# Grouping an expert's token transposes by the rows that they read

## The chip, the cores and the metric

The kernel runs on one core of one Trainium2 chip. The metric is the device time of one execution in microseconds (us). TensorE (PE) multiplies and transposes, with its weight loads recorded apart (PEld); VectorE (DVE) and ScalarE (ACT) read its results out of PSUM; GpSimd (POOL) issues the gathers and scatters; SyncE (SP) issues the large loads.

## The reference

One decoder layer over 2048 tokens of width 1024: attention and a gated recurrence side by side, an output projection, and then a sparse layer of 32 experts. Each token goes to two experts. For an expert with weights `w_gate`, `w_up` (1024 x 512) and `w_down` (512 x 1024):

```
hid = silu(xb @ w_gate[e]) * (xb @ w_up[e])
y   = (hid @ w_down[e]) * gate
out[token] += y
```

Everything is float32. Only the expert layer is touched by the change.

## The kernel before, in words

The first 1375 us or so are projections, attention, the recurrence and the routing. The rest, `phase_c`, walks over the 32 experts in an order `E[0]`, `E[1]`, ... that is fixed by `even_order`: expert number r of the size ranking has room for `CAPS[r]` tokens. Nineteen of the 32 entries of `CAPS` are over 128 (from 132 to 192), thirteen are 128. `E[0]` has 176. So `E['tails']` is one block of 128 rows for thirteen experts, and for nineteen a block of 128 rows and a second block of w = `CAPS[r]` - 128 rows, from 4 to 64.

For each expert these things happen, and the lines are those of the profile:

- `expert_in` (L1687): POOL gathers the tokens' rows from memory, the first 128 into `xg0` and the w behind them into `xg1`. Each of these tiles has one buffer, so a gather waits until the transposes of the expert before have read it. `E[0]` alone takes buffers of the name `eH`.
- `expert_x` (L1701 to L1706): PE transposes the rows, 128 columns at a time, eight such blocks (`KT` = 8) of each tile, into a PSUM tile `tr` of one bank with two buffers. ACT copies it into `xs` (L1704), DVE subtracts that from the bank to get the rest (L1705), and makes the bf16 copy `xb` (L1706). All three are needed by the expert's matmuls.
- `weights_up` (L1645, L1654, L1660) and `weights_down` (L1676): SP loads twelve pieces of 512 KB; the eight of gate and up land in `eraw` (six buffers), ACT makes `eH` of each and DVE the rest `eL` (eleven buffers each).
- `expert_up`: the gate and up matmuls, in four quarters. For an expert of over 128 tokens the weights are the stationary operand (L1727, L1724), otherwise the tokens are (L1745 to L1747).
- `expert_hid`, `expert_down`, `expert_out` (L1764, L1777 or L1789, L1822, L1829): the down projection, transposes back for the larger experts, and a scatter that adds into memory.

The order of PE's instructions is written out by hand: `manual_schedule` keeps them in the order in which the program issues them. After each quarter of `expert_up(E[r])` one step of the outstanding `expert_out` and one step of `expert_x(E[r + 1])` are issued, so the transposes of the next expert lie between the quarters of the present one:

```
for _ in self.expert_up(E[r]):
    next(out, None)
    next(x, None)
for _ in x:
    pass
```

Then come the gather of the expert after next, the down projection of the expert before, and the loads of weights. ACT, DVE, POOL and SP are ordered by the framework's planner, by the program's order, with the expert functions moved up by 250 places (`soon`), and by its own estimate of when an operand is there.

Of the kernel before, what the change touches and what calls it, by code (L numbers as in the profile page):

```python
# [9 lines left out]
F32 = mybir.dt.float32  # L10
# [5 lines left out]
AF = mybir.ActivationFunctionType  # L16
# [7 lines left out]
KT = DM // 128  # L24
# [140 lines left out]
class Layer:  # L165
# [1525 lines left out]
    @soon  # L1691
    def expert_x(self, E):
        nc, cap = self.nc, E['cap']
        xs = E['xs'] = self.mx.tile([128, KT, 2, cap], F32R, name="xs", bufs=2)
        xb = E['xb'] = self.mx.tile([128, KT, cap], BF16, name="xb", bufs=2)
        for k2 in range(KT // 2):
            pt = self.psm.tile([128, 2, 256], F32, name="tr", bufs=2)
            for j in range(2):
                k = 2 * k2 + j
                for i, w in E['tails']:  # L1700
                    nc.tensor.transpose(pt[:, j, 128 * i:128 * i + w], E['xg'][i][:, 128 * k:128 * k + 128],  # L1701
                                        self.c['ident'][0:w, 0:w])
            ks = slice(2 * k2, 2 * k2 + 2)
            nc.scalar.activation(xs[:, ks, 0, :], pt[:, :, 0:cap], AF.Copy)  # L1704
            nc.vector.tensor_sub(xs[:, ks, 1, :], pt[:, :, 0:cap], xs[:, ks, 0, :].bitcast(F32))  # L1705
            nc.vector.tensor_copy(xb[:, ks, :], xs[:, ks, 0, :].bitcast(F32))  # L1706
            yield

    @soon
# [212 lines left out]
```

## Time and profile before

| | |
|---|---|
| time, median of 3 runs | 2245.28 us (2243.73 to 2248.41) |
| the profiled execution | 2245.75 us, span 2243.9 us |
| mean granted clock of PE | 0.946 of full |
| PE | 2000.7 us busy (89%), 13777 instructions |
| PEld | 1356.6 us (60%) |
| DVE | 1500.7 us (67%), 4211 instructions |
| ACT | 1209.6 us (54%), 2691 instructions |
| POOL | 545.0 us (24%) |
| memory | 305.30 MB read, 66.29 MB written |

Busy times are shares of the whole span and mix stages with different limits. In the page's forty slices of some 56 us PE reads 9 or more from the 26th to the 38th, and DMA reads 8 or 9 there, while DVE and ACT read 5 to 7. A busy PE is not PE at its peak, since the ends of its pipelined instructions are modelled; what it could have left out is read from the distances between starts.

### The profile page before, as it was taken

To read this page: it belongs to the slowest core of one execution; us is meant where nothing else is said; L and a number is where in the kernel's file an instruction comes from. 1 tells how busy PE (TensorE), PEld (TensorE's weight loads), DVE (VectorE), ACT (ScalarE), POOL (GpSimd) and SP (SyncE) were. 2 spreads that over 40 slices of the span, in tenths; PEclk is the share of its full clock that TensorE was granted. 3 is DMA by queue.
4 is the path that set the end of the run, shared out by engine and by line. 5 is a ranking of instruction groups with operands and counts; after the bars stand their busy time and mean duration, and the time that the engine had idled before them with its cause. 6 is when DMAs were issued, how large, how long until landed. Compare 5 with 4: busy or idle time off the path is not lost. (4 is left out here: it accounts for less than half of the span.)

```text
span 2243.9 us, 39874 instructions
## 1 busy us (share of the span) xinstructions
PE 2000.7 (89%) x13777; PEld 1356.6 (60%) x13777; DVE 1500.7 (67%) x4211; ACT 1209.6 (54%) x2691; POOL 545.0 (24%) x620
## 2 busy tenths in 40 slices
PE   5998978999899998998888896999999999999981
PEld 4645565555755557554544444779999977766750
DVE  7657686778767696568876677665566656556525
ACT  6455653765547555666653433645555555555524
POOL 2312244033522235213331113021122321111110
PEclk9998988999999999999899996999999999999995
DMA  7234254533445235634579995899888999999857
GB/s 232 79 94 103 62 128 108 120 87 77 117 109 135 56 92 144 155 90 112 121 213 251 268 226 167 297 300 291 298 286 280 314 314 302 313 343 310 287 149 297
DMA packets 438896, 433.37 MB, mean 193 GB/s; under 512 B 242644, under 2 KB 325716, under 8 KB 438176
## 3 DMA queue, kind: packets, MB, share of 16 engines
q1 hardware_dynamic: 420464, 382.74, 55.8%
q0 software_dynamic: 14064, 46.46, 8.7%
q8 instruction: 108, 1.77, 0.3%
q10 hardware_dynamic: 4160, 1.58, 0.3%
q14 instruction: 100, 0.82, 0.1%
HBM read 305.30 MB, written 66.29 MB: 166 GB/s over the span
## 5 line engine op out<-in xcount | busy, mean ns | idle before, releaser
L1660 DVE TENSOR_TENSOR eL<-eraw,eH 128x1024 bf16<-128x1024 f32 x248 | 297.8, 1220 | 120.0 <-ACT eH L1654 114.5
L1654 ACT ACTIVATE eH<-eraw 128x1024 fp32r<-128x1024 f32 x252 | 258.5, 1053 | 110.5 <-PE acc L1746 59.0
L453 ACT ACTIVATE P<-S,orow,fqk 128x256 f32<-128x256 f32 (+1 forms) x384 | 195.2, 513 | 172.7 <-DVE orow L447 87.4
L567 PE MATMUL proj<-whh,x 128*128 128x512 f16 x512 | 202.6, 396 | 0.1
L568 PE MATMUL proj<-whl,x 128*128 128x512 f16 x512 | 201.2, 393 | 0.0
L569 PE MATMUL proj<-whh,x 128*128 128x512 f16 x512 | 199.9, 390 | 0.0
L1727 PE MATMUL acc<-xs,eH 128*128 128x352 f32 (+15 forms) x1216 | 196.0, 314 | 0.5 <-DVE xs L1705 0.5
L436 PE MATMUL S<-k,qs 128*128 128x256 f16 (+1 forms) x768 | 171.9, 355 | 14.1 <-ACT P L453 11.4
L1727 PEld LDWEIGHTS acc<-xs,eH 128*128 128x128 f32 x1216 | 176.1, 190 | 4.4 <-issue 2.4
L440 DVE CUSTOM_DVE_ANT_0 S<-S,bias 128x256 f32<-128x256 f32 (+1 forms) x384 | 141.3, 368 | 53.9 <-PE S L436 50.6
L456 DVE TENSOR_TENSOR Ps<-P,Ps 128x256 f16<-128x256 f32 (+1 forms) x192 | 130.6, 680 | 68.0 <-ACT Ps L455 65.1
L1829 POOL DMA_INDIRECT x2d<-yo,sidx x49 | 83.8, 1711 | 378.7 <-ACT xs L1704 98.1
L1777 PE MATMUL acc<-hs,eD 128*128 128x176 f32 (+15 forms) x1216 | 165.9, 296 | 1.1 <-DVE ts L1752 0.7
L1777 PEld LDWEIGHTS acc<-hs,eD 128*128 128x128 f32 x1216 | 160.5, 190 | 2.0 <-DVE ts L1752 1.0
L436 PEld LDWEIGHTS <-qs 128*128 128x128 f16 x768 | 89.2, 123 | 70.4 <-issue 22.8
L260 POOL TENSOR_TENSOR wraw<-wraw,g 128x1024 f32<-128x1024 f32 x44 | 84.8, 1929 | 167.2 <-DMA wraw<-in_w_in_dram 150.6
L1687 POOL DMA_INDIRECT xg<-h2d,gidx x49 | 54.7, 1117 | 268.8 <-PE tr L1701 249.0
L1745 PE MATMUL acc<-eH,xs 128*128 128x512 f32 x208 | 119.3, 574 | 0.0
L1789 PE MATMUL acc<-eD,hs 128*128 128x512 f32 x208 | 99.3, 616 | 20.5 <-ACT hs L1765 9.9
L386 PE MATMUL proj<-wh,x 128*128 128x128 f16 x512 | 95.0, 229 | 19.2 <-DVE V L394 19.2
L455 ACT ACTIVATE Ps<-P 128x256 f16<-128x256 f32 (+1 forms) x192 | 102.8, 535 | 6.0 <-DMA PT<-Ps 3.3
L658 POOL TENSOR_SCALAR sw<-Sp,hw 128x128 f32<-128x128 f32 x112 | 53.5, 478 | 197.0 <-DVE Sp L661 107.6
(396 smaller groups left out, 4960.4 us busy)
## 6 DMA issues: line engine op xcount, KB each, us to landing
eraw<-in_w_gate_dram SPq DMA_DIRECT2D x128, 512.0 KB
eD<-in_w_down_dram SPq DMA_DIRECT2D x128, 512.0 KB
eraw<-in_w_up_dram SPq DMA_DIRECT2D x124, 512.0 KB
wraw<-in_w_in_dram SPq DMA_DIRECT2D x41, 512.0 KB
od<-orow SPq DMA_DIRECT2D x64, 132.0 KB
R<-od SPq DMA_DIRECT2D x64, 132.0 KB
xt<-in_x_dram SPq DMA_DIRECT2D x16, 512.0 KB
wraw<-in_w_out_dram SPq DMA_DIRECT2D x16, 512.0 KB
```

Of the source, the lines that this page charges most:

```text
L436: nc.tensor.matmul(ps[:, h, :W], q, self.block_cols(D['k'][h][:, x], br, blk, True), start=(x == 0), stop=(x == 1))
L440: nc.vector.tensor_tensor_reduce(ps[:, h, :W], ps[:, h, :W], bias[:, 256 - W:256], 1.0, -3.0e38, OP.add, OP.max, mx[:, h:h + 1])
L453: nc.scalar.activation(P[:, h], ps[:, h, :W], AF.Exp, bias=nm[:, h:h + 1], scale=f[:, h:h + 1], accum_out=orow[:, 130 + h:131 + h])
L456: nc.vector.tensor_tensor(hv[:, 1], P, hv[:, 0], op=OP.subtract)
L567: nc.tensor.matmul(ps, self.XH[n // 4][:, k, ns], W['whh'][:, k, :], start=(k == 0), stop=False)
L568: nc.tensor.matmul(ps, self.XH[n // 4][:, k, ns], W['whl'][:, k, :], start=False, stop=False)
L569: nc.tensor.matmul(ps, self.XL[n // 4][:, k, ns], W['whh'][:, k, :], start=False, stop=(k == KT - 1))
L1654: nc.scalar.activation(H, raw, AF.Copy)
L1660: (nc.gpsimd if on_pool else nc.vector).tensor_sub(L, raw, H.bitcast(F32))
L1727: nc.tensor.matmul(gu[:, i, 0:2 * cap], w[:, o:o + 128], xs[:, k], start=(k == 0), stop=False, skip_group_check=True)
L1745: nc.tensor.matmul(gu[:, j], xs[:, k, 0], H[:, fs], start=(k == 0), stop=False)
L1777: nc.tensor.matmul(py[:, j, 0:cap], W['w_down', f][:, o:o + 128], hs[:, f], start=(f == 0), stop=(f == 3))
```

## The change

`expert_x` issues the same sixteen (or eight) transposes in another order and puts them into PSUM in other groups. Before there were four steps; each took two of the eight blocks of columns, and for each block the 128 rows and then the w rows behind them. Now there are two steps of four blocks of the first 128 rows, and for experts of over 128 tokens a third step with all eight blocks of the w rows. Each step is evicted by one ACT and two DVE instructions, as before. The element counts are the same.

```
-        for k2 in range(KT // 2):
-            pt = self.psm.tile([128, 2, 256], F32, name="tr", bufs=2)
-            for j in range(2):
-                k = 2 * k2 + j
-                for i, w in E['tails']:
-                    nc.tensor.transpose(pt[:, j, 128 * i:128 * i + w], E['xg'][i][:, 128 * k:128 * k + 128],
-                                        self.c['ident'][0:w, 0:w])
-            ks = slice(2 * k2, 2 * k2 + 2)
-            nc.scalar.activation(xs[:, ks, 0, :], pt[:, :, 0:cap], AF.Copy)
-            nc.vector.tensor_sub(xs[:, ks, 1, :], pt[:, :, 0:cap], xs[:, ks, 0, :].bitcast(F32))
-            nc.vector.tensor_copy(xb[:, ks, :], xs[:, ks, 0, :].bitcast(F32))
+
+        for i, w, k0, n in [(0, 128, 0, 4), (0, 128, 4, 4)] + [(i, w, 0, KT) for i, w in E['tails'][1:]]:
+            pt = self.psm.tile([128, n, w], F32, name="tr", bufs=2)
+            for k in range(n):
+                kk = k0 + k
+                nc.tensor.transpose(pt[:, k], E['xg'][i][:, 128 * kk:128 * kk + 128], self.c['ident'][0:w, 0:w])
+            ks, cs = slice(k0, k0 + n), slice(128 * i, 128 * i + w)
+            nc.scalar.activation(xs[:, ks, 0, cs], pt, AF.Copy)
+            nc.vector.tensor_sub(xs[:, ks, 1, cs], pt, xs[:, ks, 0, cs].bitcast(F32))
+            nc.vector.tensor_copy(xb[:, ks, cs], xs[:, ks, 0, cs].bitcast(F32))
             yield
```

## Rows read from the trace of the kernel before

**Rows 1.** Windows view: length, busy PE, PEld, DVE, ACT, POOL, clock, DMA, GB/s
```profile
1500.00:1820.00 320.00, 320.00 (x2730) 293.98 (x2728) 198.00 (x302) 180.71 (x299) 70.30 (x49) 1.00 0.91 298
...
1993.00:2015.40 22.40, 20.89 (x91) 11.57 (x89) 13.99 (x21) 12.10 (x18) 5.23 (x4) 1.00 1.03 344
```

**Rows 2.** Waits of PE from 1440 to 2140: total us, times, longest
```profile
PE acc L1789 <- ACT yo L1802: 9.4, 11, 1.5
```

**Rows 3.** Waits of ACT from 1440 to 2140
```profile
ACT eH L1654 <- PE acc L1746: 55.4, 64, 5.0
...
ACT eH L1654 <- DMA eraw<-in_w_gate_dram: 10.5, 9, 3.2
```

**Rows 4.** Timeline (start, us, engine, line): a step with w = 40
```profile
1857.47 0.90 PE L1701 MATMUL tr<-ct,xg 128*128 128x128 f32 x4
1858.30 0.50 PE L1745 MATMUL acc<-eH,xs 128*128 128x512 f32 x1
...
1857.67 0.57 PEld L1701 LDWEIGHTS tr<-ct,xg 40*128 40x128 f32 x3 [0.28 <-issue]
```

**Rows 5.** Timeline of PE: a step of an expert of 128
```profile
1899.29 0.38 PE L1701 MATMUL tr<-ct,xg 128*128 128x128 f32 x2
1899.43 0.48 PE L1745 MATMUL acc<-eH,xs 128*128 128x512 f32 x1
```

**Rows 6.** Timeline of PE: steps with w = 4, then w = 64
```profile
1706.00 0.84 PE L1701 MATMUL tr<-ct,xg 128*128 128x128 f32 x4
1706.77 2.57 PE L1727 MATMUL acc<-xs,eH 128*128 128x312 f32 x16
...
2092.03 0.93 PE L1701 MATMUL tr<-ct,xg 128*128 128x128 f32 x4
2092.89 0.50 PE L1745 MATMUL acc<-eH,xs 128*128 128x512 f32 x1
```

**Rows 7.** Timeline of PE: runs of one kind (64 rows, 32 rows, bf16)
```profile
190.78 1.71 PE L683 MATMUL hg<-qT,key 64*128 64x128 f32 x16 [0.80 <-ACT qT L674]
192.42 0.23 PE L471 MATMUL O<-V,PT 128*128 128x128 f16 x1
...
1375.76 0.63 PE L1390 MATMUL pl<-R,ctr 32*128 32x32 f32 x2
...
1378.31 0.42 PE L1402 MATMUL pl<-R,cc 32*128 32x32 f32 x1
...
1829.12 1.32 PE L1724 MATMUL acc<-xb,eL 128*128 128x164 bf16 x16
1830.28 0.60 PE L1822 MATMUL tr<-ct,yT 128*128 128x128 f32 x4
```

**Rows 8.** Groups by shape from 1320 on: count, busy us, mean ns
```profile
L1705 DVE TENSOR_TENSOR xs<-tr,xs 128x256 fp32r<-128x256 f32 x52 | 21.7, 418 | 5.2 <-ACT xs L1704 5.2
L1704 ACT ACTIVATE xs<-tr 128x256 fp32r<-128x256 f32 x52 | 19.2, 370 | 3.8 <-PE tr L1701 3.8
...
L1752 DVE TENSOR_TENSOR ts<-acc,ts 128x512 f32<-128x512 f32 x13 | 8.9, 686 | 14.0 <-ACT ts L1751 14.0
...
L1765 ACT ACTIVATE hs<-tr 128x512 f32<-128x512 f32 x13 | 7.8, 597 | 12.6 <-PE tr L1764 12.6
```

**Rows 9.** Timeline: the transposes of the first expert and its first matmuls
```profile
1389.28 4.63 DVE L1660 TENSOR_TENSOR eL<-pre,eH 128x1024 bf16<-128x1024 f32 x4
...
1394.96 0.95 DVE L1705 TENSOR_TENSOR xs<-tr,xs 128x352 fp32r<-128x352 f32 x2
1395.54 2.77 PE L1701 MATMUL tr<-ct,eH 128*128 128x128 f32 x8 [8.19 <-DVE xs L1705]
...
1398.23 2.13 PE L1727 MATMUL acc<-xs,eH 128*128 128x352 f32 x6
```

**Rows 10.** Timeline: the gather for the third expert, and PE's wait for it
```profile
1417.85 1.21 POOL L1687 DMA_INDIRECT xg<-h2d,gidx  x1 [23.22 <-PE tr L1701]
...
1423.44 0.41 PE L1701 MATMUL tr<-ct,xg 128*128 128x128 f32 x2 [3.09 <-DMA xg<-h2d,gidx]
```

## The prediction

> **What bounds the kernel now.** I read the profile in this order: the windows by stage, the waits of PE, the waits of ACT, and then PE's timeline around the transposes that are moved. All that changes lies in the walk over the experts, from about 1380 us to 2150 us.
>
> In 1500 to 1820 PE is recorded busy for the whole 320 us at a granted clock of 1.00, that is at 2.4 GHz, while DVE is busy 198 us and ACT 181 us [rows 1]. From 1440 to 2140 the longest entry among PE's waits is 9.4 us in 11 waits, on the eviction L1802 of another step [rows 2]; no wait there is for `xs`, `eH` or `eL`. ACT, the first engine that a piece of weights meets, waits 55.4 us for PE to give back `eH` buffers, and only 10.5 us for a piece to land [rows 3]. So the weights are ahead of PE, and PE's instruction stream sets the pace. A change that shortens ACT's or DVE's work is worth nothing here; one that shortens PE's stream is worth all that it saves, as far as the weights keep up.
>
> DMA is near, though: its engines are busy 0.91 of that stretch [rows 1]. But one expert's turn, 1993 to 2015.4, took 22.4 us at a DMA share of 1.03 [rows 1], so the loads can keep such a pace. The mean turn is 24 us (the 770 us above over 32 experts).
>
> **The change part by part: PE.** No transpose is added or removed. What changes is which follows which. Today a step of an expert of over 128 tokens is four transposes: 128 rows, w rows, 128 rows, w rows. From the first one's start to the next matmul's start it takes 0.83 us at w = 40 [rows 4], 0.77 us at w = 4 and 0.86 us at w = 64 [rows 6]. A step of an expert of 128, two transposes of 128 rows, takes 0.14 us [rows 5]. The moved elements don't explain this: w = 4 moves a sixteenth of w = 64 and costs nearly the same. What the row of PEld shows is that the load for the w rows stands idle 0.28 us first [rows 4], though nothing that the profile knows holds it: the weight loads, which otherwise run ahead of the matmuls, don't run ahead where the number of rows changes.
>
> The Trainium skill, page "TensorEngine Tiling (Array Packing)", section "Tiling Modes", says that a change of the tiling mode drains TensorE. The trace agrees, by the idle 0.28 us above; the sum below uses the trace's steps alone.
>
> The nineteen experts with a second block are `E[0]`, which I take apart, and 18 others. Their w are 4 to 64 with a mean of 25 (from `CAPS`), and between the 0.77 and 0.86 us that gives a mean step of 0.80 us. So the two w transposes of a step cost 0.80 - 0.14 = 0.66 us. How much of that is the transposes themselves? A run of sixteen with 64 rows and 128 columns of float32, the nearest thing in the trace, starts at 190.78 and the next kind starts at 192.42: 1.64 / 16 = 0.10 us each, the last way out included [rows 7]; two with 32 rows take 0.63 us at a granted clock of half, where a single one takes 0.42 [rows 7], so 0.21 us from start to start, which at the full clock would be about 0.11. I take 0.11 us. Two of them are 0.22, and 0.66 - 0.22 = 0.44 us of each step is for two trips into the w rows and out again, 0.22 us a trip.
>
> Before, an expert makes eight such trips (four steps, two each). After, it makes one: eight transposes of 128 rows in two groups, then eight of w rows in a run. Saved: 7 x 0.22 = 1.54 us an expert, and 18 x 1.54 = 27.7 us. For the 13 experts of 128 PE executes the same transposes in the same sequence, in two groups of four instead of four of two: nothing saved, nothing lost.
>
> The trace holds no run of w transposes, so I bound it. Were each as quick as the bf16 matmuls in a run, (1830.28 - 1829.12) / 16 = 0.073 us [rows 7], a run would be 0.3 us shorter, and the 18 experts would save 33 us. Were nothing of the weight load hidden inside the run, each would cost what an instruction in today's mixed step costs, 0.80 / 4 = 0.20 us: the run is 8 x 0.20 + 0.1 = 1.7 instead of 8 x 0.11 + 0.22 = 1.1, and 18 x 0.94 = 17 us are saved. The 64-row and 32-row runs are the nearest in kind, so I stay at 27.7.
>
> **ACT and DVE.** Evictions go from 32 x 4 = 128 steps to 19 x 3 + 13 x 2 = 83. Single ones get longer: ACT 0.60 us instead of 0.37, DVE 0.69 instead of 0.42 [rows 8]. Per expert that is less, but both engines wait for PE, so I cost it at nothing. The cover is the weights' lead: if it were gone, a piece of weights could stand 0.6 + 0.69 us behind a group. Buffers of `tr` stay two; the last group now goes out one or two quarters before the next expert needs it, where it went out in the last quarter.
>
> **The first expert.** `E[0]`'s transposes run with nothing beside them and at half clock. Today the third step waits 8.19 us for DVE to read the first one's bank, since DVE's queue has the splits of weights from 1389.28 ahead of it; it goes at 1395.54, and the matmuls begin at 1398.23 [rows 9]. After, the first two groups need only the first gather, and the third waits for the first group's bank in the same way. New is that no matmul can start before the third group is evicted, since each `xs[:, k]` now has its w columns from that group. If the planner leaves DVE's order, that costs its own eviction, some 1 us, and with one piece of weights before it on ACT and DVE up to 2.5 us. If the earlier group makes it put L1705 ahead of the four splits (4.63 us), some 4.5 us are gained. I take 0.
>
> **The third expert's gather.** POOL issues it at 1417.85, after `E[1]`'s last transposes, for which it had waited; PE then waits 3.09 us for it at 1423.44 [rows 10]. `E[1]` has 128 rows, so its transposes will end after the second quarter rather than the fourth, the gather goes out two quarters earlier, and this wait goes. Late next are the weights: this is the start, and PE would run into pieces that are not split. I take 1.5 us of the 3.09, with 0 and 3.1 as ends. Later gathers also go earlier; PE waits for none of them. SP's loads stay where they are, behind the buffers that PE frees; POOL's scatters stand behind the gathers, and get their turn sooner.
>
> **The sum.** 27.7 + 1.5 + 0 = 29.2 us. The profiled execution took 2245.75 us, its span 2243.9 and 1.85 around it, which I leave; it is 0.5 us above the median of the runs. 2245.75 - 29.2 - 0.5 = 2216 us. The ends: 33 + 3.1 + 4.5 = 40.6 us saved gives 2205; 17 + 0 - 2.5 = 14.5 saved gives 2231. That is the likeliest case's own range.
>
> **The rivals.**
>
> *Loads in a run of the same rows don't hide.* Then the upper end of the run's price holds: 17 + 1.5 saved, 2227 us. For it: in the mixed steps no load hides. Against it: the 64-row run at 0.10 us each [rows 7]. The Trainium skill, "TensorE: Matmul & The Clock Gate", section "Part 3: Packing small matmuls", says that a weight load overlaps matmuls in flight only where its row group differs, which speaks for this rival, since the eight w transposes share their rows; the 64-row run, mostly on the same rows, says otherwise. 8 in 100.
>
> *The weights take the pace.* DMA's share is 0.91 now [rows 1], and a turn shorter by 1.54 of 24 us would raise it to 0.97. If gathers and scatters among the loads keep it from going over some 0.935, a turn shrinks by 24 x (1 - 0.91 / 0.935) = 0.64 us, 18 turns save 11.6, and the time is about 2234. For it: ten microseconds of ACT's waits are for pieces already. Against it: the turn at 1.03. 10 in 100.
>
> *Longer evictions in front of the pieces.* The place is ACT's and DVE's queues, in the planner's order. A group of 512 columns holds a piece up by 0.60 + 0.69 = 1.29 us [rows 8]. If one such delay an expert reaches PE, 31 x 1.29 = 40 us come on, 40 - 29 = 11 remain, and the time is 2256, slower. It decides from 29 / 31 = 0.95 us of new waiting an expert on. For it: ACT and DVE work in order, and an expert of over 128 tokens needs four of its eight pieces in its first quarter. Against it: today no PE wait is for a piece, and ACT waits 55.4 us for PE. 8 in 100.
>
> *The saving does not reach the end.* The trips are shorter in PE's rows, and PE stands idle instead somewhere later, behind a wait that the full stream hides now: 2245. That the order on PE is not changed at all is excluded, as it is written by hand. 4 in 100.
>
> **How the numbers follow.** The forecast has 70 in 100. A measurement of this kernel tells about 0.2%, 4.5 us, from no change. Faster: 70 + 8 + 8 of the weights' 10 = 86. Within: 2 of these 10, the 4 of the last rival and 1 of the slower one's 8 = 7. Slower: 7. The range goes from 2207, a little inside the forecast's lower end, to 2236, which takes in the weights' rival.
>
> **What would show it.** In the changed kernel's PE rows, L1701 with w rows stands in runs of eight that last some 1.0 to 1.1 us up to the next matmul, and the steps of four with 128 rows last 0.36 us; the turns in the middle are 1.5 us shorter each; ACT has 83 rows of L1704. The run's length decides between the forecast and its first rival. The DMA share and ACT's waits for `eraw` decide on the second, PE's waits at L1727 and L1745 on the third. The 3.09 us for the gather are gone. The forecast is wrong if turns that host experts with a second block keep their length, or if PE's waits in 1440 to 2140 grow by over 10 us.

## The result, and the profile after

The changed kernel took 2214.4 us (median of four runs, 2210.8 to 2218.1), the kernel before 2246.9 beside it (2243.7 to 2249.4). The ratio is 0.985, with a 95% interval from 0.983 to 0.987. In two later comparisons it came to 2211.2 us (ratio 0.983, from 0.981 to 0.985) and 2211.8 us (0.984, from 0.982 to 0.986). So the change makes the kernel 1.5 to 1.7% faster: the medians lie 32, 39 and 36 us apart. The forecast was 2216, with a range from 2207 to 2236.

The windows of the changed kernel show the same 320 us that [rows 1] showed of before, then two single turns (columns as there):

```profile
1500.00:1820.00 320.00, 319.71 (x2896) 304.39 (x2897) 207.14 (x293) 189.17 (x306) 91.75 (x52) 1.00 0.95 316
1942.33:1965.90 23.57, 22.44 (x125) 17.15 (x125) 12.76 (x14) 11.78 (x15) 2.75 (x2) 1.00 0.90 310
1823.63:1847.87 24.24, 22.70 (x132) 17.11 (x133) 13.47 (x16) 11.96 (x16) 4.41 (x3) 1.00 0.98 329
```

PE is as busy as before, but executes 2896 matmuls in this stretch where it executed 2730 (2846 and 2875 in the two later profiles; the stretches do not hold exactly the same part of the walk), and DMA's share is 0.95 where it was 0.91. In the two single turns below it PE is idle for 1.1 and 1.5 us; they are taken up further down.

PE's and ACT's waits of the changed kernel from 1440 to 2110 (total us, times, longest), to be set beside [rows 2, 3]:

```profile
PE acc L1788 <- ACT yo L1801: 11.5, 11, 2.2
PE acc L1776 <- DVE ts L1751: 3.0, 3, 1.2
PE acc L1776 <- ACT yT L1778: 1.5, 1, 1.5
...
ACT eH L1654 <- PE acc L1745: 47.6, 58, 5.0
ACT eH L1654 <- DMA eraw<-in_w_gate_dram: 33.9, 23, 4.3
...
ACT yo L1801 <- DMA x2d<-yo,sidx: 9.2, 3, 3.8
```

ACT now waits 33.9 us for pieces of weights to land, three times the 10.5 of before. The lead of the weights has shrunk, and a little of that reaches PE. (`acc` is the PSUM tile of the matmuls, with three buffers. `yo` takes the result of the down projection, `yT` the same result before it is transposed back for an expert of over 128 tokens, and `ts` the product of gate and up of an expert of 128.)

PE's timeline around a run of w = 4, then one of w = 48, and a step of four blocks of 128 rows:

```profile
1716.79 0.49 PE L1821 MATMUL tr<-ct,yT 128*8 128x128 f32 x3
1717.21 0.65 PE L1701 MATMUL tr<-ct,xg 4*128 4x4 f32 x8
1717.79 0.63 PE L1726 MATMUL acc<-xs,eH 128*128 128x264 f32 x3
...
1906.23 0.69 PE L1701 MATMUL tr<-ct,xg 48*128 48x48 f32 x8
1906.85 0.50 PE L1744 MATMUL acc<-eH,xs 128*128 128x512 f32 x1
...
1415.96 0.60 PE L1701 MATMUL tr<-ct,xg 128*128 128x128 f32 x4
1416.31 2.83 PE L1726 MATMUL acc<-xs,eH 128*128 128x352 f32 x16
```

From start to next matmul the eight transposes of 4 rows take 0.58 us, those of 48 rows 0.62, and the step of four 0.35, where one mixed step of four took 0.77 to 0.86 [rows 4, 6]. The single starts within a run are 0.060 to 0.064 us apart, whatever w is, after a first one of 0.08 to 0.11; those of 128 rows are 0.109 apart.

**Where the time came from.** I cut the expert walk into turns, from the first gate-and-up matmul of one expert to that of the next, and set the two profiles side by side. Turn i hosts the steps of `E[i+1]`'s matmuls and of `E[i+2]`'s transposes; turn 0 takes in the matmuls of `E[0]` as well.

```
                                       us less than before
to the first matmul of E[0]                   -0.35
turn 0 (E[0] and E[1])                         5.07
16 turns that host a second block             30.79   (1.78 to 2.19 each)
turns 1 and 17, which host one too             0.46, 0.23
turns 19, 22, 23, 26, which host none         -0.35, -1.30, -0.46, -0.50
the other turns that host none                -0.14
from the last expert's start to the end        1.67
sum, first gather to end                      35.1    (867.57 to 832.44)
```

The spans differ by 28.6 only, since in the profile of the changed kernel the first gather happened to start 6.5 us later (1382.89 against 1376.38). Nothing before it is touched by the change, and in the two later profiles of the same kernel it starts at 1375.27 and 1380.54. Such a drift is why the experiments below are read by their turns as well as by their times. In the two later profiles the 16 turns gain 30.5 and 29.7 us.

### The profile page after: what moved, and what is told of

Its sections match the earlier page's. It is cut to its first block, busy times and chain, and to the rows that moved or that the text cites. A ratio compares the mean times of both kernels' runs of the same rounds, so it can differ in the third digit from the quotient of the medians.

```text
span 2215.3 us, 39749 instructions
## 1 busy us (share of the span) xinstructions
PE 1967.0 (89%) x13753; PEld 1345.8 (61%) x13777; DVE 1493.8 (67%) x4121; ACT 1201.4 (54%) x2646; POOL 567.3 (26%) x620
## 3 DMA queue, kind: packets, MB, share of 16 engines
q8 instruction: 109, 1.79, 0.3%
## 5 line engine op out<-in xcount | busy, mean ns | idle before, releaser
L1828 POOL DMA_INDIRECT x2d<-yo,sidx x49 | 105.2, 2146 | 255.7 <-DVE yo L1803 95.8
```

## The experiments

Each time is set beside the kernel before on the same chip, which took 2248.55 us for the first four experiments, 2250.71 for the next three kernels and 2248.26 for the last three. Where chips differ, ratios are compared.

**Pairs.** The kernel before, with the blocks inside each of its four steps ordered 128, 128, w, w instead of 128, w, 128, w. Groups and evictions are unchanged, and four trips an expert remain instead of eight.

```
-            for j in range(2):
-                k = 2 * k2 + j
-                for i, w in E['tails']:
+            for i, w in E['tails']:
+                for j in range(2):
+                    k = 2 * k2 + j
                     nc.tensor.transpose(...)
```

> The kernel before, but inside each of its four steps the two transposes of 128 rows come first and then the two of w rows (128, 128, w, w instead of 128, w, 128, w). Evictions, banks, the place of the steps and the time of the gathers stay. Theory (what costs is each change of the row count on PE): four trips into the w rows per expert instead of eight; a step falls from 0.80 to about 0.109 + 0.203 + 0.07 + 0.15 = 0.53 us, 4 x 0.27 = 1.1 us an expert and 18 x 1.1 = 19 us in all: about 2227 us. Rival (the gain comes from fewer and larger evictions, or from the steps that end earlier): no change, 2247 within 4 us.

It took 2226.7 us, ratio 0.991 (0.989 to 0.994), as the theory forecast. A step of w = 4 in its timeline of PE:

```profile
1704.04 0.59 PE L1701 MATMUL tr<-ct,xg 128*128 128x128 f32 x4
1704.56 0.61 PE L1777 MATMUL acc<-hs,eD 128*128 128x136 f32 x3
```

The step takes 0.52 us where it took 0.77 [rows 6], and the same 16 turns are 0.95 to 1.18 us shorter each. Order alone, with the same instructions and evictions, so gives half of the gain: four trips fewer are worth about 1 us, 0.25 to 0.26 us a trip.

**Wide.** The kernel before in its own order, but the second block lies in a 128-row tile that was cleared once, and all 128 rows of it are transposed. No change of rows remains (but in `E[0]`, whose tiles stay as they were), at the price of transposing rows that nobody reads.

```
+                if 'x1' not in self.__dict__:
+                    self.x1 = self.mx.tile([128, DM], F32, name="xg1")
+                    nc.vector.memset(self.x1, 0.0)
+                x = self.x1[0:w]
...
+                    w = E['xg'][i].shape[0]
                     nc.tensor.transpose(pt[:, j, 128 * i:128 * i + w], E['xg'][i][...],
                                         self.c['ident'][0:w, 0:w])
```

> The kernel before in its own order (128, w, 128, w), but the second block's tile is one of 128 rows, cleared once, and it is transposed with all 128 rows, so that no instruction of a step changes the row count; only the first w columns of the result are read. Theory (changes of the row count cost): the four starts of a step are 0.109 us apart, the step takes 0.36 instead of 0.80 us, 4 x 0.44 = 1.8 us an expert, 18 x 1.8 = 32 us, of which some 4 to 6 are given back in the turns that wait for weights: 2215 to 2222 us, though the wait for the third expert's gather stays. Rival (turning to and fro between two gathered tiles, or small results in one bank, is what costs): 2247 within 4 us.

It took 2216.8 us, ratio 0.986 (0.984 to 0.989). Its steps of four take 0.35 us, as this row of PE's timeline and the next show:

```profile
1709.74 0.60 PE L1707 MATMUL tr<-ct,xg 128*128 128x128 f32 x4
1710.09 2.18 PE L1733 MATMUL acc<-xs,eH 128*128 128x264 f32 x16
```

The 16 turns gain 29.5 us in sum, nearly what they gain in the changed kernel (30.8), though the order is that of before and more rows are transposed. So it is the change of the number of rows that costs, and neither the transposes nor the grouping of evictions. A transpose of w rows also streams only w columns of the identity, and this experiment undoes both. But a mere change in the columns streamed is seen to cost nothing: two transposes of 128 columns between matmuls of 512 take 0.14 us [rows 5]. Few columns without few rows were not tried.

**Early.** The kernel before, with the transposes of the second expert two steps a quarter; so only the third expert's gather goes out sooner.

```
                             next(x, None)
+                            if r == 0:
+                                next(x, None)
```

> The kernel before, but the four steps of the second expert (128 rows) are issued two a quarter, so that they end after the second quarter and the third expert's gather goes out two quarters earlier. Nothing else moves. Theory (the wait of 3.1 to 3.4 us on the gather goes, and with it the 3.4 us at half clock behind it, 1.7 us): 5 us less, 2242. Rival 1 (PE runs into pieces of weights instead, as forecast): 1 to 2 us less. Rival 2: no change.

It took 2244.3 us, ratio 0.998 (0.996 to 1.000). That is 4 us less, just about what can be told. The profile is clearer: turn 0 is 4.81 us shorter, and the 16 turns 0.00 in sum. So most of the changed kernel's 5.07 us in turn 0 are the gather's. The other turns show how far two profiles of the old order can differ: their lengths agree within 0.02 us, except 19, 23 and 26, which are 0.28 and 0.68 shorter and 0.40 longer than in the profile of the kernel before, though nothing was changed there. Why turn 0 gains more than the 3.09 us of the wait [rows 10] can be seen in the windows of the kernel before just after it (columns as in [rows 1]):

```profile
1420.00:1424.00 4.00, 0.91 (x6) 0.53 (x5) 3.03 (x4) 1.72 (x3) 0.00 (x0) 1.00 0.99 383
1424.30:1427.70 3.40, 3.40 (x10) 1.80 (x8) 2.90 (x4) 1.06 (x1) 0.00 (x0) 0.50 1.04 410
```

and in those of the changed kernel at its end of the first turn:

```profile
1420.00:1430.00 10.00, 10.00 (x64) 7.46 (x63) 8.86 (x12) 8.17 (x11) 0.00 (x0) 1.00 0.87 321
```

Before, PE stood idle for 3.1 us, worked on at the full clock from 1423.44 to 1424.30, and then worked 3.4 us at a granted clock of 0.50, that is at 1.2 GHz, before it was back at 2.4 GHz. The work of these 3.4 us at half clock would take 1.7 at the full one: 3.1 + 1.7 = 4.8 us, which is what this experiment gained. In the changed kernel and in this experiment there is neither the wait nor the slow stretch. The Trainium skill, "TensorE: Matmul & The Clock Gate", section "Part 1: The HAM clock gate", describes a clock that falls on an idle engine and comes back under load; the two rows agree.

**Halves.** The changed kernel with each group evicted in two halves on ACT and DVE: 166 evictions of ACT instead of 83, and none is longer than it was before the change.

```
+            for h in range(2):
+                hn = slice(n // 2 * h, n // 2 * h + n // 2)
+                ks = slice(k0 + hn.start, k0 + hn.stop)
-            nc.scalar.activation(xs[:, ks, 0, cs], pt, AF.Copy)
+                nc.scalar.activation(xs[:, ks, 0, cs], pt[:, hn], AF.Copy)
...
```

> The changed kernel, with each bank evicted in two halves by two ACT and four DVE instructions: 166 evictions instead of 83, more than the 128 of the kernel before. PE's order stays as in the changed kernel. Theory (evictions are beside the path): as the changed kernel, 2214 within 4 us. Rival (fewer evictions were part of the gain): some 0.2 us a half on ACT and 0.3 on DVE, up to 83 x 0.5 = 41 us on the path in the worst case; at least 5 us slower than the changed kernel, 2219 or more.

It took 2222.4 us, ratio 0.988 (0.985 to 0.991), some 7 us over the changed kernel's 0.985, though the intervals overlap; its walk from the first gather on is 837.4 us long, 3.0 to 6.8 more than in the three profiles of the changed kernel. I had expected no difference, and the rival's 2219 us or more came true. The reason is not that fewer evictions were part of the gain ("pairs" and "wide" gain with 128 of them); it stands among PE's waits from 1440 to 2110:

```profile
PE tr L1701 <- DVE yo L1806: 5.2, 5, 1.1
...
PE tr L1701 <- PE tr L1824: 3.1, 4, 0.8
```

PE now waits for a free `tr` bank, which it never did before in this stretch. Turns 15, 20 and 27 lose all of their 2 us, and the 16 turns gain 24.8 instead of 29.7 to 30.8. So the evictions lie beside the path only as long as two banks hold; fewer and longer ones are no burden here, more and shorter ones are.

**The changed kernel again,** as a base on the next chip:

> The changed kernel once more, as the base for the two kernels beside it. Both theories: 2214.4 us as before, 2211 to 2218, 0.985 of the kernel before (interval within 0.983 to 0.987). In its profile the six turns whose host is an expert of 128 slots (blocks 1, 17, 19, 22, 23, 26) should again give back some 5 to 6 us in sum, if that loss is a property of the kernel and not of the one profile.

It took 2211.2 us, and in its profile the six turns 1, 17, 19, 22, 23 and 26 come to +0.2 us in sum where they came to -1.9 in the first one, and -3.1 in the third. If turns 1 and 17 gained 1.9 each and the rest nothing, the sum would be 3.8, so 3.6 to 6.9 us are given back there, 3.6 in this profile where 5 to 6 were expected. Size and place vary with the run, and 22, 23 and 26 lose in all three. Against "early" instead of the one profile of the kernel before, 26 loses no more than 0.06 to 0.35 us, and 23 loses 0.84 to 1.14. The largest single case is turn 17 of the first profile:

```profile
1836.83 4.62 PE L1776 MATMUL acc<-hs,eD 128*128 128x164 f32 x32
1841.06 1.06 ACT L1654 ACTIVATE eH<-eraw 128x1024 fp32r<-128x1024 f32 x1 [4.34 <-DMA eraw<-in_w_gate_dram]
1842.02 0.58 ACT L1750 ACTIVATE ts<-acc 128x512 f32<-128x512 f32 x1
...
1842.49 0.77 ACT L1778 ACTIVATE yT<-acc 128x328 f32<-128x328 f32 x2
...
1842.98 1.80 PE L1776 MATMUL acc<-hs,eD 128*128 128x164 f32 x11 [1.54 <-ACT yT L1778]
```

These are rows of the timeline. ACT stands 4.34 us behind a split whose piece has not landed. The evictions L1750 and L1778 are queued behind it though PE has long finished what they read, and PE, out of banks, waits 1.54 us for the second one. PE's row names ACT; the cause is the piece two lines above. Two experiments ask why it is late.

**Seven buffers.** The changed kernel with `RAW` (the buffers of `eraw`) 7 instead of 6.

> The changed kernel with seven buffers for weight pieces in place of six. Theory (the turns hosted by experts of 128 slots give back some 5.8 us because a piece is issued too late for want of a free buffer, so that ScalarE's queue stands behind a split of a piece that has not landed): a piece is issued one piece earlier, ScalarE's waits for pieces in the expert part fall from 33.9 us to under 20, and the time falls by 3 to 6 us, to 2208 to 2211. Rival (the transfers themselves are at their rate, so an earlier issue only lengthens the queue they stand in): waits and time as in the changed kernel, 2214 within 3 us.

It took 2218.3 us, ratio 0.986 (0.984 to 0.988): 7 us longer than the changed kernel beside it, which neither side had expected. The profile says something finer. ACT's waits for pieces, 1440 to 2110, and PE's are

```profile
ACT eH L1654 <- DMA eraw<-in_w_gate_dram: 11.0, 8, 2.5
...
PE acc L1788 <- ACT yo L1801: 12.5, 11, 2.0
PE acc L1776 <- DVE ts L1751: 1.5, 2, 1.1
```

ACT's waits for pieces fell to what they were in the kernel before [rows 3], from 33.9, 20.5 and 32.5 us in the three profiles of the changed kernel; turn 17 has its full 2.04 us, and turn 22 loses 0.62 instead of 1.2 to 1.6, though 26 loses as in "early" (0.37). The walk from the first gather on took 829.6 us, against 832.4, 830.6 and 834.4 of the three profiles of the changed kernel. What was won was small, and the times don't show it. The larger pool also changed the order of some instructions of ACT, DVE and SP before the expert walk, from 1188 us on; whether that made the four runs longer isn't shown, since the only profile is of the fastest of them (2210.9).

**Less weight.** The changed kernel, in which each expert of 128 tokens from the third on loads no `w_down` of its own and uses that of the expert before. This leaves out part of the computation: the outputs of those experts are others.

```
+        if E['cap'] == 128 and E['r'] != self.E[1]['r']:
+            for h in range(4):
+                E['W']['w_down', h] = self.E[self.E.index(E) - 1]['W']['w_down', h]
+            return
```

> The changed kernel without part of its loads: every expert of 128 slots from the third on does not load its w_down, and multiplies by the w_down of the expert before it instead, so the outputs of those experts differ from the reference. Every matmul, transpose and eviction stays; four pieces (and their splits on ScalarE and VectorE) of such an expert go. Theory (the weights' loads set the pace in the turns hosted by experts of 128 slots, which give back 5.8 us): ScalarE's waits for pieces fall from 33.9 us to under 10 us, the six turns keep what the other turns gain, and the time is 5.8 us or more below the changed kernel's, 2208 or less. Rival (the give-back is a matter of the order of evictions on ScalarE, with no part of the loads): the six turns stay as they are and the time is 2214 within 3 us.

It took 2208.7 us, ratio 0.982 (0.980 to 0.984), 2.6 us less than the changed kernel beside it, which is within what can be told and less than the theory's 5.8. The DMA share from 1800 to 2115 fell from 0.92 to 0.81 (windows), and ACT's and PE's waits from 1440 to 2110 read

```profile
PE acc L1792 <- ACT yo L1805: 12.8, 11, 3.0
...
ACT yo L1805 <- DMA x2d<-yo,sidx: 14.5, 4, 4.8
...
ACT eH L1654 <- DMA eraw<-in_w_gate_dram: 11.3, 10, 2.7
```

Turn 17 has its 2.04 us, turn 22 loses nothing, turn 26 even gains 0.98. But turn 23 still loses 0.39 and turn 1 now loses 2.04, and every wait of PE that is left is for `yo`. So late pieces explain turns 17 and 22, and the waits of 26 (there without the change too), and not 1 and 23. That turn 1 even lost 2 us is one wait of PE and the clock behind it, as this row of the timeline and this one of the windows show:

```profile
1467.89 2.97 PE L1792 MATMUL acc<-eD,hs 128*128 128x512 f32 x4 [3.04 <-ACT yo L1805]
...
1468.75:1472.16 3.41, 3.41 (x8) 1.76 (x7) 0.00 (x0) 0.41 (x1) 0.54 (x1) 0.50 1.03 411
```

PE waits 3.04 us for `yo` and then works 3.4 us at half clock, 1.7 us more, as before the third expert's gather. My expectation that all six turns would come back was wrong. (This `w_down` is not split by ACT or DVE as the expectation says; only loads go.)

**The changed kernel a third time,** the base for the last two:

> The changed kernel a third time, as the base for the two kernels beside it: 2211 to 2215 us, a ratio to the kernel before of 0.983 to 0.986. In its profile, blocks 1 and 23 should again lose to the kernel before plus the expected gain (block 1 gains some 0.5 to 0.7 us in place of 1.8; block 23 loses 0.2 to 0.5 us), with one wait of TensorE for the eviction of yo on ScalarE of about 2 us in each.

It took 2211.8 us. Turns 1 and 23 gained 0.62 and -0.26, as expected, with one wait of PE for `yo` in each, 2.06 and 1.79 us. Turn 17 lost 1.79 where it had gained 0.23 and 0.66:

```profile
1840.59 3.73 PE L1776 MATMUL acc<-hs,eD 128*128 128x164 f32 x16 [1.90 <-ACT yT L1778]
...
1841.68:1845.07 3.39, 3.39 (x16) 3.34 (x15) 0.00 (x0) 0.44 (x1) 0.00 (x0) 0.50 0.65 241
```

Its wait for `yT` was 1.90 us, against 1.54 and 1.12 in the other two profiles, and here too the granted clock was 0.50 for 3.4 us behind it. The waits of about 2 us in turns 1 and 23 had no such stretch behind them, so the length of the wait alone does not decide.

**Every transpose of the run twice.**

```
+                for _ in range(1 + (n == KT)):
                     nc.tensor.transpose(pt[:, k], E['xg'][i][...], ...)
```

> The changed kernel with every transpose of the run of eight issued twice in a row, to the same place (the result is the same): 18 experts by 8 more transposes of w rows, nothing else. Theory (the steps in the trace show their true cost, 0.062 us each whatever w): 18 x 8 x 0.062 = 8.9 us, a little less where a turn has slack: 2219 to 2224 where the changed kernel stands at 2211 to 2215. Rival (the price that the prediction took, 0.11 us each as for 128 rows): 15.8 us, 2227 to 2231.

It took 2220.6 us, ratio 0.987 (0.985 to 0.989), 8.8 us more than the base beside it, where 18 x 8 x 0.062 = 8.9 were forecast and 15.8 by the prediction's price. PE's timeline for w = 4:

```profile
1697.94 1.15 PE L1702 MATMUL tr<-ct,xg 4*128 4x4 f32 x16
1699.01 0.41 PE L1727 MATMUL acc<-xs,eH 128*128 128x312 f32 x1
```

The run takes 1.07 us with sixteen transposes and 0.58 with eight: 0.49 / 8 = 0.061 us each. The 16 turns' mean gain falls from 1.92 in the first profile of the changed kernel to 1.44 us, by the same 0.49.

**Two buffers for yo.** The changed kernel with one more buffer of `yo0`. Every engine executes the same instructions in the same order.

```
-            E['yo'] = self.mx.tile([128, DM], F32, name="xg1" if E is self.E[-2] else "yo0")
+            E['yo'] = self.mx.tile([128, DM], F32, name="xg1" if E is self.E[-2] else "yo0",
+                                   bufs=1 if E is self.E[-2] else 2)
...
-                yo = self.mx.tile([w, DM], F32, name=f"yo{i}")
+                yo = self.mx.tile([w, DM], F32, name=f"yo{i}", bufs=2 - i)
```

> The changed kernel with two buffers in place of one for the outputs of the first 128 slots (yo0). Theory (blocks 1 and 23 give back some 1.3 and 0.3 us because ScalarE's eviction of yo waits up to 3.8 us for the scatter that still reads the one buffer, and TensorE then waits 2.0 us for that eviction): ScalarE's 9.2 us of waits for the scatter go, the two blocks regain 1 to 2 us in sum, and the time falls by as much, to 2209 to 2213. That is about the size of what a comparison can tell, so the blocks in the profile decide. Rival (the eviction is late because a piece's split stands before it in ScalarE's queue, whatever the buffer): the wait of TensorE stays, time and blocks as in the changed kernel.

It took 2209.5 us, ratio 0.983 (0.981 to 0.986). PE's waits from 1440 to 2110:

```profile
PE acc L1789 <- ACT yo L1802: 8.9, 11, 1.1
PE acc L1776 <- DVE ts L1751: 2.4, 2, 1.6
PE acc L1776 <- ACT yT L1778: 1.9, 1, 1.9
```

No wait for `yo` is longer than 1.1 us where the longest in the base was 2.1, and ACT's waits for the scatter are gone from its list. Turn 1 gains 1.91 (0.62 in the base) and turn 23 gains 0.75 (-0.26), 2.3 us together; turn 17 loses 1.79 as in the base, since its cause is a piece (PE's wait is 1.89 us, and the clock falls behind it again). So the theory holds for these two turns. The time, 2.3 us below the base, agrees but could not have told it alone. Its ratio is no lower than the changed kernel's lowest (0.983), so a faster kernel is not shown. This buffer and the seventh of `eraw` were not tried together.

## Why the prediction was right

**The bound.** PE's stream set the pace, as predicted: "pairs" and "wide" shorten nothing else, and their turns follow PE's rows.

**The saving of the trips** was forecast at 18 x 1.54 = 27.7 us. The mechanism was right, and the term too small: 16 of the 18 turns gained 1.92 us on average, 30.8 in sum. The step that was mis-sized is the price of a transpose of w rows in a run, 0.11 us; it is 0.062, below even the bound of 0.073 that I took from bf16 matmuls. Neither of the two rows that it was taken from is a transpose of w rows: both are matmuls, one with 128 columns and one at half clock, where two starts are 0.21 us apart by the prediction's count. The 48-row transposes of `E[0]`, which run at half clock in the changed kernel, start 0.107 us apart there. A run lasts 0.58 to 0.64 us and not 1.0 to 1.1, so the first sign that I named for my step failed, on the favourable side. At the right price a trip costs more: with 0.062 each, (0.66 - 0.12) / 2 = 0.27 us instead of 0.22, and 7 x 0.27 = 1.9. The Trainium skill, "TensorE: Matmul & The Clock Gate", section "Back-to-back issue gap", gives about 62 ns a matmul for moving counts from 1 to 64 in one of its two modes of decoding. The trace agrees with that figure (0.060 to 0.064 from w = 4 to w = 64), and I had passed it over.

One reading was weaker than I took it for. The 0.28 us for which a load of w rows stands idle [rows 4] is no sign of a change by itself, since a load in a step of 128, where no number of rows changes, stands idle as long in the kernel before:

```profile
1899.06 0.10 PEld L1747 LDWEIGHTS <-xb 128*128 128x128 bf16 x1 [0.28 <-issue]
```

There a matmul of 512 columns runs meanwhile. What shows the price is the distance between PE's starts: 0.20 to 0.26 us from 128 rows to the w rows behind them in a mixed step, where 128 rows follow 128 at 0.109.

**The first rival,** that loads on the same rows don't hide, is refuted by the same rows. The statement of the Trainium skill that the prediction cites for it ("TensorE: Matmul & The Clock Gate", section "Part 3: Packing small matmuls"), that a load overlaps only where the row group differs, does not hold for these runs: a load takes 0.13 to 0.14 us, and the transposes start 0.062 apart.

**The third expert's gather** was put at 1.5 us and brought about 4.8 ("early"). The wait went whole, and with it the stretch at half clock behind it, a term that the prediction left out though the clock is in the profile's rows. That the weights would be late next at this place was wrong.

**The first expert** was put at 0, between a loss of 2.5 and a gain of 4.5; it lost 0.35 us (0.34 and 0.35 in the repeats). These rows of the timeline answer to [rows 9]:

```profile
1400.34 1.22 DVE L1660 TENSOR_TENSOR eL<-eraw,eH 128x1024 bf16<-128x1024 f32 x1
1401.48 1.28 DVE L1704 TENSOR_TENSOR xs<-tr,xs 128x512 fp32r<-128x512 f32 x2
...
1402.22 1.09 PE L1701 MATMUL tr<-ct,eH 48*128 48x48 f32 x8 [11.38 <-DVE xs L1704]
...
1405.09 2.13 PE L1726 MATMUL acc<-xs,eH 128*128 128x352 f32 x6 [1.78 <-DVE xs L1704]
```

DVE still splits weights ahead of the bank that PE waits for, and the new wait for the third group's own eviction is there (1.78 us), as described. It is paid for by the earlier end of the transposes.

**The weights' rival** was partly true. DMA's share rose to 0.95 where it was to rise to 0.97 by the forecast and to stay under 0.935 by the rival. The 16 turns lost little: 29.7 to 30.8 us remain. The loss came instead in turns whose host is an expert of 128 tokens, where late pieces (17, 22) and a single `yo` buffer (1, 23) are the main part of the 3.6 to 6.9 us given back, with 1.7 of them the clock's in the third profile. The forecast had no term for that. Its two small terms (6.8 us too little over 18 experts, 3.3 at the gather) and this missing one cancel in part, so a median 2 us from the forecast says less than it seems. Not forecast either was 1.7 us at the end, most of it in the last expert's one wait of PE for L1764 on ACT, 8.5 us where it was 9.9.

**The slower rival,** evictions in front of pieces, did not happen: ACT's longer evictions cost no turn of the 16, and halving them made it worse. **That the saving does not reach the end** is refuted by the times.

Of the other signs, ACT has its 83 evictions (at L1703 in the changed kernel), and PE's waits grew from 10.5 to 16.0 us, less than the 10 us more that would have spoken against the forecast.

What stays open: why PE waited 0.76 us in turn 19 of the first profile, which lost 0.35 us, and not at all in both repeats, which gained 0.67; when the clock falls behind a wait of some 2 us and when not; and why the kernel with seven buffers took longer in three of its four runs.

## What to carry to other kernels

Look for small matmuls or transposes that alternate between numbers of rows, and count the changes and not the elements: issue those of one kind together, or pad the small ones where no order is free. When PE's stream gets shorter, look next at the queue of the engine that evicts: one instruction there that waits for a transfer holds up evictions whose data are ready, and PE's row names the wrong culprit. Count a stretch at half clock behind a wait as part of what the wait costs.

## What the runs showed of the hardware

Float32 transposes in a run start 0.060 to 0.064 us apart from 4 to 64 rows and 0.109 us apart at 128, with the loads hidden in both (a load takes 0.13 to 0.14 us). A change from 128 rows to w rows and back costs about a quarter of a microsecond beside that, 0.27 by the steps and 0.25 to 0.26 by "pairs". After idle stretches of 3.1 us (before), 3.04 ("less weight") and 1.9 (the third profile of the changed kernel), PE worked on for about a microsecond at 2.4 GHz, then for 3.4 us at 1.2, before it was granted 2.4 again; after one of 2.23 us (turn 1 of the first profile) it stayed at 2.4.
